# A decoder trunk in float32: the MLP's down projection as a 2x2 block product with seven products

## The chip, the cores and the metric

The kernel is one program on one core of a Trainium2 chip. The core has a tensor engine (PE) with a weight load queue (PEld), a vector engine (DVE), a scalar engine (ACT), a general engine (POOL), and a queue that issues DMAs (SP). The metric is device microseconds of one execution. The kernel before took 1333.41 us, the median of three runs (1332.4 to 1335.83).

## What is computed

Two decoder layers on 512 tokens of width 1024. A layer is a token mixer, an MLP and a gated per-layer embedding:

```
for i in range(2):
    hn = rmsnorm(h, norm_mix_g[i])
    h = h + (even_mixer if i == 0 else odd_mixer)(hn, ...)
    hn = rmsnorm(h, norm_mlp_g[i])
    u = square(relu(hn @ w_mlp_up[i]))       # 512 x 4096
    h = h + u @ w_mlp_down[i]                # 512 x 1024
    gate = sigmoid(rmsnorm(h, norm_ple_g[i]) @ w_ple_gate[i])
    h = h + (p[i] @ w_ple_proj[i]) * gate
return rmsnorm(h, final_norm_g)
```

Everything is float32. The change is in the line with `w_mlp_down`, and in where a few tiles of the other stages lie.

## The kernel before

Activations are kept transposed: eight tiles `h0` to `h7` of 128 features x 512 tokens. Every large product is done in float32r with both operands split into a high and a low part, three matmuls for each pair of 128x128 weights and moving tile (`mm3`): high x high, high x low, low x high. The weights come as 1 MB blocks (`wload`, two buffers `raw`); ACT makes the high part (`wh`, a copy into float32r), DVE the low part (`wl`, the difference), three buffers of 128 x 1024 each. In the mixers POOL makes the low parts instead.

The MLP goes over the hidden width in four chunks of 1024. In a chunk, four *up blocks* each make two hidden tiles of 128 x 512: 48 matmuls of 512 columns into two PSUM banks, then relu and the norm's factor on DVE (L674), the square on ACT (L675), the high part on ACT (L678) and the low part on DVE (L679). Then four *down blocks* each make two tiles of the output: for each tile eight k-steps of `mm3`, 48 matmuls of 512 columns, and DVE adds the bank to `h` (L686). In the last chunk each finished tile is handed on to the next norm (`nxt.done`: split, square, running sum). PSUM has eight banks, taken in turn.

Each engine works its instructions off in the order that the framework's scheduler has put them in when the kernel is built; that order is fixed, and an instruction that waits holds up those behind it on its engine. SP issues the weight blocks in the order of use, each waiting until its `raw` buffer is free. A pool's memory is given to the next pool when the first one closes, and the first writer there waits for the last reader.

The per-layer embedding's projection is computed during the mixer, stored to DRAM (`pjd`) and read back as eight tiles `pj`; before, the pool for them is opened ahead of the MLP, so that these loads stand in front of the MLP's second weight block. The mixer uses scratch tiles `tmp` and `tmp2` and four half-zero tiles `klz`, which before live for the whole kernel.

Of the kernel before, what the change touches and what calls it, by code (L numbers as in the profile page):

```python
# [19 lines left out]
P = 128  # L20
D = 1024
S = 512
# [40 lines left out]
def trunk(  # L63
# [8 lines left out]
    def nm(s):  # L72
        uid[0] += 1
        return f"{s}_{uid[0]}"
# [8 lines left out]
    def const(shape, name, dtype=F32):  # L83
        return cpool.tile(shape, dtype, tag=name, name=name)

    T_BUFS = {"e": 5, "tmp": 1, "tmp2": 3}

    def t2k(tag, pool=None, dtype=F32):
        return (pool or spool).tile([P, S], dtype, tag=tag, name=nm(tag), bufs=T_BUFS.get(tag, 2))

    def col(name="c"):
        return spool.tile([P, 1], F32, tag="col", name=nm(name), bufs=24)
# [9 lines left out]
    def ps_wide():  # L102
        t = ps(wide[wide_i[0] % 8])
        wide_i[0] += 1
        return t
# [45 lines left out]
    def run(units):  # L151
        for _ in units:
            pass
# [204 lines left out]
    klz = [[const([P, S], f"klz{s}{x}", F32R) for x in range(KLB)] for s in range(2)]  # L358
    kl_i = [0]
    for x in range(KLB):  # L360
        nc.gpsimd.memset(klz[0][x][64:128].bitcast(F32), 0.0)
        nc.gpsimd.memset(klz[1][x][0:64].bitcast(F32), 0.0)


    def mixer(layer, norm, nxt):
        st = ExitStack()
        mpool = st.enter_context(tc.tile_pool(name=f"mpool{layer}", bufs=2))
        NSLOT = 13
        pth = [mpool.tile([P, NSLOT, P], F32R, tag=f"pth{i}", name=nm("pth"), bufs=1) for i in range(2)]
        ptl = [mpool.tile([P, NSLOT, P], F32R, tag=f"ptl{i}", name=nm("ptl"), bufs=1) for i in range(2)]  # L370
# [286 lines left out]
        st.close()  # L657


    def mlp(layer, fpool, norm, nxt):  # L660
        ahl = norm.parts()
        rstd = None
        NCH = 4
        for ch in range(NCH):
            uhl = []
            for c in range(4):
                blk = block(w_up[layer, 4 * ch + c], KT, P)
                accs = [ps_wide() for _ in range(2)]
                run(lin_units(accs, blk, ahl, 0, KT, ch == 0 and c == 0))
                if rstd is None:  # L670
                    rstd = norm.finish(use_tables(sig_tail) if layer == 0 else None)
                for acc in accs:
                    u = t2k("u", fpool)
                    nc.vector.scalar_tensor_tensor(u, acc, 0.0, rstd, op0=ALU.max, op1=ALU.mult)  # L674
                    nc.scalar.activation(u, u, AF.Square, scale=0.5)  # L675
                    uh = fpool.tile([P, S], F32R, tag="uh", name=nm("uh"), bufs=12)
                    ul = fpool.tile([P, S], F32R, tag="ul", name=nm("ul"), bufs=12)
                    nc.scalar.activation(uh, u, AF.Copy)  # L678
                    nc.vector.tensor_tensor(ul, u, uh.bitcast(F32), op=ALU.subtract)  # L679
                    uhl.append((uh, ul))  # L680
            for c in range(4):
                blk = block(w_down[layer, 4 * ch + c], KT, P)
                for i in range(2):
                    acc = ps_wide()
                    lin(acc, blk[i][0], blk[i][1], uhl, 0, KT)
                    nc.vector.tensor_tensor(h[2 * c + i], h[2 * c + i], acc, op=ALU.add)  # L686
                    if ch == NCH - 1:
                        nxt.done(2 * c + i)


    def ple_proj(layer, pool):
# [110 lines left out]
    for layer in range(DEPTH):  # L802
        n_mlp, n_ple, n_next = Norm(1, layer), Norm(2, layer), Norm(0, layer + 1)
        mixer(layer, norm, n_mlp)
        with tc.tile_pool(name=f"ppool{layer}", bufs=1) as ppool:
            lo_eng[0] = nc.vector
            pj = ple_proj(layer, ppool)
            with tc.tile_pool(name=f"fpool{layer}", bufs=1) as fpool:
                mlp(layer, fpool, n_mlp, n_ple)
            with tc.tile_pool(name=f"gpool{layer}", bufs=1) as gpool:  # L810
                if layer < DEPTH - 1:
                    ple_t(layer, gpool, pj, n_ple, n_next)
                else:
                    ple_final(layer, gpool, pj, n_ple)
        norm = n_next
        lo_eng[0] = nc.gpsimd


def _pack(w, rows, c0, n, subs, split_rows=False):

    t = np.stack([w[r * P:(r + 1) * P, c0:c0 + n] for r in rows], axis=1)
    if split_rows:
        t = t.reshape(P, subs, len(rows) // subs, n)
    else:
        t = t.reshape(P, len(rows), subs, n // subs).transpose(0, 2, 1, 3)
    return t.reshape(P, -1)


def _feeds(a):
# [3 lines left out]
    for layer, w in enumerate((a["w_in_even"][0], a["w_in_odd"][0])):  # L833
        blocks = []
        for j, g in enumerate(GROUPS[layer]):
# [4 lines left out]
            else:  # L840
# [20 lines left out]
        "w_down": np.array([[_pack(down[l], range(8 * ch, 8 * ch + 8), 256 * c, 256, 2)  # L861
                             for ch in range(4) for c in range(4)] for l in layers]),
# [31 lines left out]
```

## Time and profile before

| | |
|---|---|
| median of three runs | 1333.41 us |
| profiled execution | 1334.15 us, span of the core 1332.4 us, granted clock 0.997 |
| layer 0: mixer, MLP, gate | to about 299 us, to about 647 us, to about 699 us |
| layer 1: mixer, MLP, gate and output | to about 937 us, to about 1273 us, to the end |
| DMA | 133.07 MB, mean 100 GB/s |

The page gives each engine's busy time and its share of the span; the chain of waits follows the work that ended last back from the end; a group of instructions has its line, engine, shapes, count, total busy time and mean duration in ns, and then the idle time before it with what ended it. Durations of matmuls overlap on PE, so the distance from start to start in the timeline is read beside them.

### The profile page before, as it was taken

The page shows a single profiled execution, that of the slowest core. Times are in us where ns is not written, and L with a number is a line of the kernel's source. Part 1 is how long each engine was busy: PE and PEld are TensorE (multiplying, and loading weights), DVE is VectorE, ACT ScalarE, POOL GpSimd, SP SyncE. Part 2 cuts the span into 40 slices and gives each one's busy share as a digit, 9 for nine tenths or more (in the row PEclk, how much of TensorE's full clock was granted, in tenths as well). Part 3 has the DMA queues.
Part 4 walks back from the last instruction along what each step waited for, and adds up shares of the span by engine and source line. Part 5 has one row for each costly group of instructions (what it writes and reads, how often), then busy time and mean ns, then how long its engine had stood idle before and what let it go on. Part 6 is the DMA issues. An engine that isn't in the chain of part 4 may idle for free.

```text
span 1332.4 us, 16447 instructions
## 1 busy us (share of the span) xinstructions
PE 1302.0 (98%) x6360; PEld 1089.0 (82%) x6360; DVE 804.8 (60%) x1389; ACT 631.9 (47%) x1085; POOL 187.2 (14%) x156
## 2 busy tenths in 40 slices
PE   8999999999999999999999999999999999999997
PEld 7878787788888888888889899878888888888886
DVE  6688789865344343345667888887634434434566
ACT  6566768544233132234456667765422313324344
POOL 2333343410000000000004333322000000000001
PEclk9999999999999999999999999999999999999999
DMA  5321323243222222222232232214322222222221
GB/s 205 116 95 56 111 96 104 87 158 111 103 102 95 95 95 95 95 95 95 95 119 99 71 109 74 70 64 148 105 97 97 101 104 102 100 96 95 95 79 64
DMA packets 28031, 133.07 MB, mean 100 GB/s; under 512 B 3312, under 2 KB 4048, under 8 KB 15280
## 3 DMA queue, kind: packets, MB, share of 16 engines
q1 hardware_dynamic: 27952, 132.01, 28.8%
q8 instruction: 50, 0.82, 0.3%
q14 instruction: 29, 0.24, 0.1%
HBM read 125.63 MB, written 6.37 MB: 99 GB/s over the span
## 4 chain that ended last, share of the span: by engine, by line
PE 77%; DVE 14%; ACT 6%; issue 1%; DMA 1%; SPq 0%; ACTq 0%
PE mm L135 12%; PE mm L134 12%; PE mm L136 12%; PE tp L134 5%; PE tp L136 5%; PE tp L135 5%; PE sc L134 5%; PE sc L136 5%; PE sc L135 5%; PE pv L135 3%; PE pv L134 2%; PE pv L136 2%; DVE e L568 2%; PE pv L530 2%; DVE qq L463 1%
## 5 line engine op out<-in xcount | busy, mean ns | idle before, releaser
L120 ACT ACTIVATE wh<-raw 128x1024 fp32r<-128x1024 f32 (+1 forms) x216 | 224.7, 1043 | 497.6 <-PE mm L135 180.4
L134 PE MATMUL mm<-hi,wh 128*128 128x512 f32 x564 | 222.4, 394 | 0.5 <-ACT wh L300 0.4
L124 POOL TENSOR_TENSOR wl<-raw,wh 128x512 fp32r<-128x512 f32 (+1 forms) x132 | 176.5, 1360 | 322.4 <-ACT wh L120 315.8
L135 PE MATMUL mm<-lo,wh 128*128 128x512 f32 x564 | 221.0, 392 | 0.3 <-DVE lo L175 0.3
L136 PE MATMUL mm<-hi,wl 128*128 128x512 f32 x564 | 220.5, 391 | 0.3 <-DVE wl L126 0.3
L126 DVE TENSOR_TENSOR wl<-raw,wh 128x1024 fp32r<-128x1024 f32 x150 | 183.4, 1224 | 44.1 <-ACT wh L120 37.8
L136 PEld LDWEIGHTS mm<-hi,wl 128*128 128x128 f32 x564 | 106.0, 188 | 23.4 <-DVE wl L126 0.7
L134 PEld LDWEIGHTS mm<-hi,wh 128*128 128x128 f32 x564 | 106.1, 188 | 20.7 <-ACT wh L300 0.7
L135 PEld LDWEIGHTS mm<-lo,wh 128*128 128x128 f32 x564 | 106.1, 188 | 20.6 <-DVE lo L175 1.0
L507 ACT ACTIVATE e<-e,mn 128x128 f32<-128x128 f32 (+3 forms) x96 | 53.8, 561 | 52.8 <-DVE mn L504 52.4
L134 PE MATMUL mm<-uh,wh 128*128 128x512 f32 x192 | 74.7, 389 | 0.0
L135 PE MATMUL mm<-ul,wh 128*128 128x512 f32 x192 | 74.7, 389 | 0.0
L136 PE MATMUL mm<-uh,wl 128*128 128x512 f32 x192 | 74.7, 389 | 0.0
L136 PE MATMUL sc<-hi,wl 128*128 128x512 f32 x168 | 65.6, 390 | 0.0
L135 PE MATMUL sc<-lo,wh 128*128 128x512 f32 x168 | 65.4, 389 | 0.0
L134 PE MATMUL sc<-hi,wh 128*128 128x512 f32 x168 | 65.4, 389 | 0.0
L135 PE MATMUL mm<-wl,hi 128*128 128x256 f32 (+1 forms) x216 | 64.6, 299 | 0.4 <-DVE wl L126 0.4
L136 PE MATMUL mm<-wh,lo 128*128 128x256 f32 (+1 forms) x216 | 64.4, 298 | 0.0
L134 PE MATMUL mm<-wh,hi 128*128 128x256 f32 (+1 forms) x216 | 64.3, 298 | 0.0
L780 POOL TENSOR_TENSOR ht<-ht,gb 128x512 f32<-128x512 f32 x4 | 6.3, 1596 | 390.0 <-ACT gt L778 390.0
L686 DVE TENSOR_TENSOR h<-h,mm 128x512 f32<-128x512 f32 x24 | 16.5, 688 | 72.7 <-PE mm L136 72.7
L134 PE MATMUL tp<-hi,wh 128*128 128x512 f32 x152 | 59.1, 389 | 0.0
(218 smaller groups left out, 2883.5 us busy)
## 6 DMA issues: line engine op xcount, KB each, us to landing
raw<-in_w_up_dram SPq DMA_DIRECT2D x32, 1024.0 KB, 4.8
raw<-in_w_down_dram SPq DMA_DIRECT2D x32, 1024.0 KB, 4.9
raw<-in_w_in_dram SPq DMA_DIRECT2D x23, 1024.0 KB, 4.9
raw<-in_w_gate_dram SPq DMA_DIRECT2D x8, 1024.0 KB, 4.9
bias<-urow SPq DMA_DIRECT2D x24, 256.0 KB, 3.2
raw<-in_w_outa_dram SPq DMA_DIRECT2D x8, 768.0 KB, 4.3
pjd<-tmp SPq DMA_DIRECT2D x16, 256.0 KB, 2.3
pj<-pjd SPq DMA_DIRECT2D x16, 256.0 KB, 4.2
```

What stands on the lines that cost most here:

```text
L120: nc.scalar.activation(hi, src, AF.Copy)
L124: nc.gpsimd.tensor_tensor(lo[:, kx], src[:, kx], hi[:, kx].bitcast(F32), op=ALU.subtract)
L126: nc.vector.tensor_tensor(lo, src, hi.bitcast(F32), op=ALU.subtract)
L134: nc.tensor.matmul(acc, lh, rh, start=start, stop=False)
L135: nc.tensor.matmul(acc, lh, rl, start=False, stop=False)
L136: nc.tensor.matmul(acc, ll, rh, start=False, stop=stop)
L463: nc.vector.tensor_tensor(q[b], f[a], q[a].bitcast(F32), op=ALU.subtract)
L507: nc.scalar.activation(e[:, 0:n], e[:, 0:n], AF.Exp, scale=-1.0, bias=mn, accum_out=s)
L530: nc.tensor.matmul(op[:, q0:S], stat(j), mov, start=c == 0, stop=c == nmm - 1)
L568: nc.vector.tensor_tensor_scan(kr, kr, kr, 1.0, op0=ALU.mult, op1=ALU.bypass)
L686: nc.vector.tensor_tensor(h[2 * c + i], h[2 * c + i], acc, op=ALU.add)
L780: nc.gpsimd.tensor_tensor(hk[t][:, 0:512], hk[t][:, 0:512], gb[:, 0:512], op=ALU.mult)
```

## The change

In the first three of the four chunks the down projection is done as a block product. The hidden tiles of one up block (two tiles of 128 features, each with a left and a right half of 256 tokens) are a 2x2 block matrix B; the weights of one down block are, for each of the four up blocks, a 2x2 matrix A of 128 x 128 blocks. Seven products replace eight:

- DVE combines the hidden halves into T1 to T4 (of the four Bs), and the weights into S1 to S4, in float32, before the split. The hidden tile of an up block becomes one tile of seven 256-column pieces (T1, B11, T3, B21, B22, T2, T4); its high and low parts are made in one instruction each. Five such tiles are kept.
- A down block makes the products S1T1, S2T2, S3T3, A11B11, S4B22, A12B21 and A22T4, with moving operands of 256 columns, each 4 x 3 matmuls, in four PSUM banks. The products that reach several outputs (S1T1, S2T2, S3T3, A11B11) are collected over the three chunks in `side` tiles (ACT copies them in the first chunk, DVE adds them in the other two); the others go into `h` at once.
- `side_sums` adds the collected products into the four output blocks, eight DVE instructions of 256 columns for each of the four column blocks, once a layer.
- The order of the blocks is now: the first up block of a chunk, the four down blocks of the chunk before, the other three up blocks. The fourth chunk's down blocks stay as they were, with eight k-steps of 512 columns.
- The host packs the weights of the changed blocks as A12, A22, A21, A11.
- `tmp`, `tmp2` and `klz` now lie in the mixer's pool (so `klz` is zeroed in each layer), and `pj` is loaded in the gate's pool, after the MLP.

The core of the diff; what is left out is marked:

```diff
     def t2k(tag, pool=None, dtype=F32):
-        return (pool or spool).tile([P, S], dtype, tag=tag, name=nm(tag), bufs=T_BUFS.get(tag, 2))
+        return (pool or (mix[0] if tag in ("tmp", "tmp2") else spool)).tile([P, S], dtype, tag=tag, name=nm(tag), bufs=T_BUFS.get(tag, 2))
...
+    T1, B11, T3, B21, B22, T2, T4 = range(7)
...
+            u = fpool.tile([P, 7, HW], F32, tag="u", name=nm("u"), bufs=1)
+            uh = fpool.tile([P, 7, HW], F32R, tag="uh", name=nm("uh"), bufs=5)
+            ul = fpool.tile([P, 7, HW], F32R, tag="ul", name=nm("ul"), bufs=5)
+            for i, acc in enumerate(accs):
+                ui = u[:, B11 + 2 * i:B11 + 2 * i + 2].rearrange("p a c -> p (a c)")
+                nc.vector.scalar_tensor_tensor(ui, acc, 0.0, rstd[0], op0=ALU.max, op1=ALU.mult)
+                nc.scalar.activation(ui, ui, AF.Square, scale=0.5)
+            parts = slice(0, 7)
+            if ch < NCH - 1:
+                nc.vector.tensor_tensor(
+                    u[:, T1:T3 + 1:2], u[:, B11:B22 + 1:3], u[:, T3:T3 + 1].to_broadcast([P, 2, HW]), op=ALU.subtract)
+                nc.vector.scalar_tensor_tensor(
+                    u[:, T2], u[:, T1], -1.0, u[:, B22], op0=ALU.mult, op1=ALU.subtract)
+                nc.vector.scalar_tensor_tensor(
+                    u[:, T4], u[:, T2], -1.0, u[:, B21], op0=ALU.mult, op1=ALU.subtract)
+            else:
+                parts = slice(B11, B22 + 1)
+            nc.scalar.activation(uh[:, parts], u[:, parts], AF.Copy)
+            nc.vector.tensor_tensor(ul[:, parts], u[:, parts], uh[:, parts].bitcast(F32), op=ALU.subtract)
...
+        def down(ch, c):
+            raw = wload(w_down[layer, 4 * ch + c])
+            rv = raw.rearrange("p (s k c) -> p s (k c)", s=4, k=4)
+            A12, A22, S3, A11 = range(4)
+            sums = fpool.tile([P, 3, S], F32, tag="sums", name=nm("sums"), bufs=1)
+            S1, S2, S4 = range(3)
+            nc.vector.tensor_tensor(sums[:, S1], rv[:, S3], rv[:, A22], op=ALU.add)
+            nc.vector.tensor_tensor(sums[:, S2], sums[:, S1], rv[:, A11], op=ALU.add)
+            nc.vector.tensor_tensor(rv[:, S3], rv[:, S3], rv[:, A11], op=ALU.add)
+            nc.vector.tensor_tensor(sums[:, S4], sums[:, S2], rv[:, A12], op=ALU.add)
...
+            def product(bank, half, w, x, t, start, stop):
+                wh, wl = w
+                acc = banks[bank][:, half * HW:half * HW + HW]
+                for k, (uh, ul) in enumerate(us):
+                    mm3(acc, wh[:, x, k], wl[:, x, k], uh[:, t], ul[:, t], start and k == 0, stop and k == 3)
...
+            w = split(sums[:, S1:S2 + 1])
+            product(0, 0, w, 0, T1, True, False)
+            product(0, 1, w, 1, T2, False, True)
+            total(0, 0)
+            w = split(rv[:, S3:A11 + 1])
+            product(1, 0, w, 0, T3, True, False)
+            product(1, 1, w, 1, B11, False, True)
+            total(1, 1)
+            product(2, 1, split(sums[:, S4:S4 + 1]), 0, B22, True, False)
+            w = split(rv[:, A12:A22 + 1])
+            product(2, 0, w, 0, B21, False, True)
+            nc.vector.tensor_tensor(h[2 * c], h[2 * c], banks[2], op=ALU.add)
+            product(3, 0, w, 1, T4, True, True)
+            nc.vector.tensor_tensor(h[2 * c + 1][:, 0:HW], h[2 * c + 1][:, 0:HW], banks[3][:, 0:HW], op=ALU.subtract)
...
+        for c in range(4):
+            up(0, c)
+        for ch in range(1, NCH):
+            up(ch, 0)
+            for c in range(4):
+                down(ch - 1, c)
+            for c in range(1, 4):
+                up(ch, c)
+                if ch == NCH - 1:
+                    side_sums(c)
+        side_sums(0)
+        for c in range(4):
+            down_last(c)
...
-        with tc.tile_pool(name=f"ppool{layer}", bufs=1) as ppool:
-            lo_eng[0] = nc.vector
-            pj = ple_proj(layer, ppool)
-            with tc.tile_pool(name=f"fpool{layer}", bufs=1) as fpool:
-                mlp(layer, fpool, n_mlp, n_ple)
-            with tc.tile_pool(name=f"gpool{layer}", bufs=1) as gpool:
...
+        lo_eng[0] = nc.vector
+        with tc.tile_pool(name=f"fpool{layer}", bufs=1) as fpool:
+            mlp(layer, fpool, n_mlp, n_ple)
+        with tc.tile_pool(name=f"gpool{layer}", bufs=1) as gpool:
+            pj = ple_proj(layer, gpool)
...
```

How this moves instructions, at three places. In the rows a name is a buffer with its number, what is written to the left of the arrow, what is read to the right.

PE in a down block of layer 0. Before, the first matmuls of the first chunk's first block (`mm_3513` is a bank, `wh_3505` and `wl_3506` the weights' parts, `uh`, `ul` those of the hidden tiles):

```order
L134 MATMUL mm_3513<-uh_3208,wh_3505 128x512
L135 MATMUL mm_3513<-ul_3209,wh_3505 128x512
L136 MATMUL mm_3513<-uh_3208,wl_3506 128x512
L134 MATMUL mm_3513<-uh_3215,wh_3505 128x512
L135 MATMUL mm_3513<-ul_3216,wh_3505 128x512
L136 MATMUL mm_3513<-uh_3215,wl_3506 128x512
```

Now, in a block of the second chunk, where one product ends and the next begins:

```order
L136 MATMUL mm_4481<-uh_4159,wh_4557 128x256
L137 MATMUL mm_4481<-ul_4160,wh_4557 128x256
L138 MATMUL mm_4481<-uh_4159,wl_4558 128x256
L136 MATMUL sc_4482<-uh_3483,wh_4557 128x256
L137 MATMUL sc_4482<-ul_3484,wh_4557 128x256
L138 MATMUL sc_4482<-uh_3483,wl_4558 128x256
```

The matmuls are half as wide, and a block has 84 instead of 48; the order on PE is otherwise that of the program.

DVE in a run of down blocks. Before, in layer 0's second chunk, low parts of weights and adds into `h` take turns:

```order
L686 TENSOR_TENSOR h_91<-h_91,pv_4021 128x512
L126 TENSOR_TENSOR wl_4112<-raw_4109,wh_4111 128x1024
L686 TENSOR_TENSOR h_92<-h_92,mm_4057 128x512
L126 TENSOR_TENSOR wl_4116<-raw_4109,wh_4115 128x1024
L686 TENSOR_TENSOR h_93<-h_93,mm_4083 128x512
```

Now, in the third chunk, between the second and the third block (`wl_5229` is the low part of the third block's first pair, `side` and L766 are the side totals and the side sums, L713 a weight sum of the fourth block):

```order
L766 TENSOR_TENSOR h_90<-h_90,side_3113 128x256
L742 TENSOR_TENSOR side_3114<-side_3114,sc_5109 128x512
L726 TENSOR_TENSOR wl_5229<-sums_5219,wh_5228 128x1024
L726 TENSOR_TENSOR e_5287<-sums_5219,e_5286 128x512
L766 TENSOR_TENSOR h_90<-h_90,side_3112 128x256
L742 TENSOR_TENSOR side_3115<-side_3115,tp_5110 128x512
L766 TENSOR_TENSOR h_91<-h_91,side_3113 128x256
L726 TENSOR_TENSOR wl_5258<-raw_5217,wh_5257 128x1024
L713 TENSOR_TENSOR sums_5334<-raw_5332 128x512
```

The low parts of the next block stand behind the side totals of the block that PE is at, and the side sums of the first column blocks are put between them rather than after the run.

SP at the end of layer 0's MLP. Before:

```order
L112 DMA raw_5476<-in_w_gate_dram 128x2048
L112 DMA raw_5560<-in_w_gate_dram 128x2048
L112 DMA raw_5644<-in_w_gate_dram 128x2048
L112 DMA raw_5750<-in_w_in_dram 128x2048
L112 DMA raw_5810<-in_w_in_dram 128x2048
```

Now:

```order
L114 DMA raw_6189<-in_w_gate_dram 128x2048
L797 DMA pj_5993<-pjd 128x512
L797 DMA pj_5995<-pjd 128x512
L797 DMA pj_5997<-pjd 128x512
L797 DMA pj_5999<-pjd 128x512
L797 DMA pj_6001<-pjd 128x512
L797 DMA pj_6003<-pjd 128x512
L797 DMA pj_6005<-pjd 128x512
L797 DMA pj_6007<-pjd 128x512
L114 DMA raw_6273<-in_w_gate_dram 128x2048
L114 DMA raw_6386<-in_w_in_dram 128x2048
```

The eight loads of `pj`, which stood ahead of the MLP's second weight block, now stand between the third and the fourth block of the gate's weights.

More of the change, by code (lines that the diff above doesn't have):

```diff
@@ L367, in mixer @@
         mpool = st.enter_context(tc.tile_pool(name=f"mpool{layer}", bufs=2))
+        mix[:] = [mpool]
+        klz = [[mpool.tile([P, S], F32R, tag=f"klz{s}{x}", name=nm("klz"), bufs=1) for x in range(KLB)]
+               for s in range(2)]
+        for x in range(KLB):
+            nc.gpsimd.memset(klz[0][x][64:128].bitcast(F32), 0.0)
+            nc.gpsimd.memset(klz[1][x][0:64].bitcast(F32), 0.0)
         NSLOT = 13
@@ L657, in mixer @@
         st.close()
+    HW = S // 2
+    T1, B11, T3, B21, B22, T2, T4 = range(7)
     def mlp(layer, fpool, norm, nxt):
         ahl = norm.parts()
-        rstd = None
+        rstd = []
         NCH = 4
-        for ch in range(NCH):
-            uhl = []
-            for c in range(4):
[L667 to L688, printed above, removed]
@@ new lines, in mlp, with up @@
+        sides = [[fpool.tile([P, S], F32, tag=f"side{x}{c}", name=nm("side"), bufs=1) for x in range(2)] for c in range(4)]
+        hidden = {}
+        def up(ch, c):
+            blk = block(w_up[layer, 4 * ch + c], KT, P)
+            accs = [ps_wide() for _ in range(2)]
+            run(lin_units(accs, blk, ahl, 0, KT, ch == 0 and c == 0))
+            if not rstd:
+                rstd.append(norm.finish(use_tables(sig_tail) if layer == 0 else None))
+            u = fpool.tile([P, 7, HW], F32, tag="u", name=nm("u"), bufs=1)
[17 more added lines that the diff above has]
+            nc.vector.tensor_tensor(ul[:, parts], u[:, parts], uh[:, parts].bitcast(F32), op=ALU.subtract)
+            hidden[ch, c] = (uh, ul)
@@ new lines, in down_last @@
+        def down_last(c):
+            blk = block(w_down[layer, 4 * (NCH - 1) + c], KT, P)
+            uhl = [tuple(x[:, B11 + 2 * i:B11 + 2 * i + 2].rearrange("p a c -> p (a c)") for x in hidden[NCH - 1, k])
+                   for k in range(4) for i in range(2)]
+            for i in range(2):
+                acc = ps_wide()
+                lin(acc, blk[i][0], blk[i][1], uhl, 0, KT)
+                nc.vector.tensor_tensor(h[2 * c + i], h[2 * c + i], acc, op=ALU.add)
+                nxt.done(2 * c + i)
```

45 lines of the change are left out of this document (35 added, 10 removed).

## The prediction

> **What bounds the kernel now.** I read the page first (busy shares, then the chain of waits), then a stretch of the MLP in the view by stages, then the timeline of TensorE, because the page warns that a busy PE is not PE at its peak.
>
> ```profile
> PE 1302.0 (98%) x6360; PEld 1089.0 (82%) x6360; DVE 804.8 (60%) x1389; ACT 631.9 (47%) x1085; POOL 187.2 (14%) x156
> PE 77%; DVE 14%; ACT 6%; issue 1%; DMA 1%; SPq 0%; ACTq 0%
> raw<-in_w_down_dram SPq DMA_DIRECT2D x32, 1024.0 KB, 4.9
> 331.00:508.00 177.00, 177.00 (x783) 146.56 (x782) 72.07 (x81) 53.03 (x65) 0.00 (x0) 1.00 0.29 100
> ```
>
> The last row is a stage wholly inside layer 0's MLP; its columns are the length, then busy time of PE, PEld, DVE, ACT and POOL, the granted clock, DMA share and GB/s. PE is busy 177.00 of 177.00 us at clock 1.00; DVE and ACT are busy 72 and 53 us, and POOL does nothing. Nothing but PE sets the time here. So the change is worth what it does to PE's time, as long as DVE and ACT, which get more work, stay behind cover. Of the 32 blocks of the down projection, 24 change (three chunks of four column blocks, two layers).
>
> The trap is the duration of a matmul. By shapes, and then as starts in the timeline (columns: start, duration):
>
> ```profile
> L136 PE MATMUL mm<-uh,wl 128*128 128x512 f32 x192 | 74.7, 389 | 0.0
> L136 PE MATMUL sc<-wh,lo 128*128 128x256 f32 x32 | 9.1, 283 | 0.0
> 339.77 0.39 PE L135 MATMUL pv<-ul,wh 128*128 128x512 f32 x1
> ...
> 349.97 0.39 PE L135 MATMUL mm<-ul,wh 128*128 128x512 f32 x1
> 39.76 0.28 PE L134 MATMUL sc<-wh,hi 128*128 128x256 f32 x1
> ...
> 44.68 0.28 PE L136 MATMUL tp<-wh,lo 128*128 128x256 f32 x1
> ```
>
> Going by durations, a 256-column matmul would cost 283/389 = 0.73 of a 512-column one. But they overlap: from 339.77 to 349.97 lie 45 steps, 226.7 ns each; from 39.76 to 44.68 lie 41 steps, 120.0 ns each. What counts is the step. Two points give a line: (226.7 - 120.0)/256 = 0.417 ns per column and 13.3 ns per matmul whatever its width. The 256-column matmuls of that stretch (the first value projection) are built as the new ones will be: a fresh 128x128 float32r stationary operand each, one bank half as target.
>
> **The change part by part.**
>
> *PE.* A changed block went through 2 accumulators x 8 k x 3 = 48 matmuls of 512 columns: 48 x 226.7 = 10.88 us. Now it goes through 7 products x 4 k x 3 = 84 of 256 columns: 84 x 120.0 = 10.08 us. In the two terms of that line: 3072 columns less at 0.417 ns save 1.28 us, and 36 more fixed costs of 13.3 ns take 0.48 back. The saving is 0.80 us a block, **24 x 0.80 = 19.2 us**. Bounds of the 120 ns: below, half of 226.7 (no fixed cost), 113.3, saving 1.36 x 24 = 32.6 us; above, the break-even is 10.88/84 = 129.5 ns, only 8% off, so this number carries the forecast. I take 120.0, the row of the same form.
>
> [...]
>
> *DVE and ACT, does the cover hold?* Prices:
>
> ```profile
> L126 DVE TENSOR_TENSOR wl<-raw,wh 128x1024 fp32r<-128x1024 f32 x150 | 183.4, 1224 | 44.1 <-ACT wh L120 37.8 <-PE tp L242 6.3
> L679 DVE TENSOR_TENSOR ul<-u,uh 128x512 fp32r<-128x512 f32 x64 | 44.1, 691 | 0.0
> L686 DVE TENSOR_TENSOR h<-h,mm 128x512 f32<-128x512 f32 x24 | 16.5, 688 | 72.7 <-PE mm L136 72.7
> L520 DVE TENSOR_TENSOR ptl<-tp,pth 128x256 fp32r<-128x256 f32 x28 | 11.5, 412 | 0.5 <-ACT pth L519 0.5
> L120 ACT ACTIVATE wh<-raw 128x1024 fp32r<-128x1024 f32 x200 | 211.2, 1059 | 496.2 <-PE mm L135 179.1 <-PE tp L135 114.5 <-PE sc L135 108.5
> L678 ACT ACTIVATE uh<-u 128x512 fp32r<-128x512 f32 x64 | 40.5, 633 | 2.0
> L675 ACT ACTIVATE u<-u 128x512 f32<-128x512 f32 x64 | 39.6, 619 | 8.8 <-DVE u L674 8.8
> ```
>
> A changed down block on DVE: four weight sums 4 x 0.69, three low parts of 1024 columns 3 x 1.22, one of 512 0.69, two side totals 2 x 0.69 (in the first chunk ACT copies them), h adds 0.69 + 0.41: 9.6 us (8.2 in the first chunk), was 3.8. ACT: 3 x 1.06 + 0.63 = 3.8 us. An up block of the first three chunks on DVE: 2 x 1.22 + 2 x 0.69, combinations 0.69 + 2 x 0.41, low part of 1792 columns, 2.02 by the slope of the first two rows: 7.4 us, was 5.2. So an up and a down block together hold 17.0 us of DVE under 20.96 us of PE. On average the cover holds; inside a run of four down blocks it is tight, 9.6 under 10.08, and the extra work of the up block before it falls there too.
>
> So I followed the queue by hand, in the order shown, through the hardest run: the third chunk's four down blocks, where the order also places the side sums (8 x 0.41 a block). T = 0 is the first of their matmuls; a product takes 12 x 0.12 = 1.44 us. A weight buffer of three is refilled when the two products that read it are over, so a pair of the next block can be split 7.2 us before PE wants it, and the split takes 1.06 (ACT) + 1.22 (DVE): 4.9 us of margin. DVE starts with the tail of the up block (relu, low part of 1024; done at 4.1). It reaches the low part of the second block's first pair at 5.9 (wanted at 10.1), of the third block's at 15.6 (20.2), of the fourth's at 26.1 (30.2), of the next up block's first half at 37.3 (40.3) and of its second at 40.3 (45.8). Margins shrink from 4.9 to 3.0 us and never reach nothing. The walk lets a DVE instruction start up to 0.08 us before its predecessor's duration is over, as these two do (1.19 us apart at 1.23 long):
>
> ```profile
> 399.77 1.23 DVE L126 TENSOR_TENSOR wl<-raw,wh 128x1024 fp32r<-128x1024 f32 x1 [0.17 <-ACT wh L120]
> 400.96 0.69 DVE L679 TENSOR_TENSOR ul<-u,uh 128x512 fp32r<-128x512 f32 x1
> 404.35 0.69 DVE L674 SCALAR_TENSOR_TENSOR u<-mm,rstd 128x512 f32<-128x512 f32 x1 [2.69 <-PE mm L136]
> ```
>
> With full durations one after another the smallest margin is about 1.9 us. So the cover costs nothing at these durations. If it goes, DVE sets the pace (below). Below nothing the edit cannot go: PE has no idle time there to win.
>
> *Last up block to first plain down block.* The last hidden tile is now made in one piece of 1024. After its last matmul: relu 0.69, ACT's weight split 1.06 beside it, square 0.62, high part 1.06, low part 1.22, about 4.1 us. PE wants the high part after 18 matmuls, 4.08 us, the low part one step later. Even; at most 0.5 us a layer. I take 0.
>
> *PLE reload.* The eight loads of pj move on SP's queue from before the MLP to after the third gate load, and wait there for the MLP's last matmul; behind them stands the fourth gate load (in layer 1 also the final gain and the last two gate loads).
>
> ```profile
> L695 SPq DMA_DIRECT2D pj<-pjd x16: 326/431/1469, 270.6 to 913.0; - x16
> L713 DVE TENSOR_TENSOR gt<-gt,pj x8: 679/684/692, 655.2 to 685.9; 128x512 f32<-128x512 f32 x8
> DMA to landing us min/median/max: 3.0/4.2/6.7
> 1279.61 4.99 SPq L112 DMA_DIRECT2D raw<-in_w_gate_dram  x2
> 1285.31 1.06 ACT L120 ACTIVATE wh<-raw 128x1024 fp32r<-128x1024 f32 x1 [6.19 <-PE tp L136]
> ```
>
> Eight issues take 8 x 0.43 = 3.5 us; the last lands 7 to 11 us after the last down matmul. The first is wanted after a gate block of PE (48 x 0.227 = 10.9 us) and the norm behind it, so it is hidden; the fourth gate load is wanted 33 us on. In layer 1 the two gate loads of 1279.61 may land some 4 us later and delay the split of 1285.31, whose weights serve the second half of the gate, after 96 x 0.227 = 22 us. 0, at most 1.5 us.
>
> *Mixer scratch and klz.* Four memsets are added on POOL at the start of layer 1, ahead of the value weights' splits:
>
> ```profile
> L361 POOL MEMSET klz<- 64x512 f32 x2 | 1.0, 520 | 0.1
> 687.75 0.35 POOL L372 MEMSET ptl<- 128x128 f32 x2
> 694.49 2.57 POOL L124 TENSOR_TENSOR wl<-raw,wh 128x512 fp32r<-128x512 f32 x2 [6.38 <-ACT wh L120]
> ```
>
> 4 x 0.52 = 2.1 us into 6.38 us in which POOL waits for ACT: 0. The scratch tiles keep their number of buffers: 0.
>
> *Sum.* The profiled execution took 1334.15 us with a span of 1332.4; the median of the runs is 1333.41, 0.7 less. 1333.4 - 19.2 = **1314.2 us**.
>
> **The rivals.** The bound of faster and slower is 0.3%, 4.0 us, about what a measurement of this kernel tells from no change.
>
> *Part of the gain is given back in stalls.* The four or six runs of down blocks eat their margin at the seams and PE waits 1 to 2.3 us in each of six: 6 to 14 us, so 1320 to 1328. For it: the margins of 1.9 to 3.0 us above come from a count by hand. Against: every run before it has more room, and up blocks leave DVE 3.5 us each to recover.
>
> *DVE becomes the bound (slower).* Place: the low parts in the down runs. In DVE's order the side totals and h adds wait for PE, and the low parts behind them wait with them. It decides once a down block takes DVE over 10.08 us, 5% above my sum, for longer than the margin lasts. Price, with nothing of it hidden by the lead: in the second chunk's run 4 x 9.6, the up block's tail 0.69 + 0.69 + 0.82 + 2.02 and the next up block's split 2.45 make 45.1 us against 40.3 of PE; in the third chunk's 4 x 9.6 + 1.9 + 2.45 and the side sums, 13.2, make 56.0. Over by 4.8 + 15.7 us a layer, 41 us in all: 1314 + 41 = 1355; half of it 1335. If the adds ran as slowly as these, it would be far more:
>
> ```profile
> L472 DVE TENSOR_TENSOR klz<-tmp,kh 64x512 fp32r<-64x512 f32 x32 | 32.8, 1025 | 8.5 <-ACT kh L470 8.2
> ```
>
> at 1.49 times 0.69, a block takes 13.1 us and 24 x (13.1 - 10.88) = +53, 1387. Those ran while POOL was at work; in the MLP POOL has x0, and L679 takes 691.
>
> *The step of a 256-column matmul is not 120 ns here.* If PE could not overlap weight loads with such short matmuls, each pair would cost its load:
>
> ```profile
> L136 PEld LDWEIGHTS mm<-hi,wl 128*128 128x128 f32 x564 | 106.0, 188 | 23.4 <-DVE wl L126 0.7
> ```
>
> 84 x 0.188 = 15.8 us a block, +118 us, 1451. Against: the stretch at 39.76 had a load per matmul too. [...]
>
> *More is saved:* a step nearer 117 or 113 ns, 1301 to 1308.
>
> **How the numbers follow.** Forecast (1308 to 1319) 0.67; stalls (1320 to 1328) 0.15; DVE bound (1329 to 1355) 0.10; a dearer step 0.03; more saved 0.05. Faster needs less than 1329.4: 0.86; within: 0.07; slower: 0.07. The range runs from 1306 to 1327.
>
> **What would show it.** PE should hold 7224 matmuls, with starts 120 ns apart in the down runs and idle under 5 us more than before; DVE about 1010 us busy (805 and 24 x 5.8 - 8 x 1.4, 24 x 2.2, 8 x 3.3); PE waits released by DVE's low parts at L726 absent. Waits there, or a step above 125 ns, would make the prediction wrong.

## The result and the profile after

The changed kernel takes 1315.14 us, the median of four runs (1313.5 to 1315.48); the kernel before, on the same chip, 1334.62 us (1332.4 to 1336.32). The ratio is 0.9853, with an interval of 0.9834 to 0.9871. The forecast was 1314.2 us. The profiled execution took 1313.5 us with a span of 1311.6; that of before had a span of 1332.4.

Two lines of the page of the changed kernel, engines and chain of waits:

```profile
PE 1280.7 (98%) x7224; PEld 1112.5 (85%) x7224; DVE 982.5 (75%) x1669; ACT 686.4 (52%) x1117; POOL 189.0 (14%) x160
...
PE 78%; DVE 12%; ACT 7%; issue 2%; DMA 1%; SPq 0%; ACTq 0%; DVEq 0%
```

DVE has 178 us more work than before and 15 points more of the span, yet its share of the chain has fallen from 14% to 12%, a first sign that the added work is not on the path. The view by stages says where it went. Its rows are the three runs of four changed down blocks in layer 0; the columns are length, busy time of PE, PEld, DVE, ACT and POOL, granted clock, DMA share and GB/s:

```profile
342.27:382.59 40.32, 40.32 (x338) 40.31 (x337) 28.50 (x35) 20.16 (x25) 0.00 (x0) 1.00 0.32 109
426.13:466.45 40.32, 40.32 (x338) 40.31 (x337) 33.83 (x43) 16.09 (x16) 0.00 (x0) 1.00 0.33 109
509.99:550.31 40.32, 40.32 (x338) 40.31 (x337) 39.31 (x66) 15.39 (x16) 0.00 (x0) 1.00 0.32 109
```

PE is busy for the whole of each run, even of the third, in which DVE is busy 39.31 us of 40.32. The same stretch of before, the four plain down blocks of the third chunk:

```profile
507.51:551.02 43.51, 43.51 (x193) 36.03 (x192) 15.97 (x17) 9.64 (x11) 0.00 (x0) 1.00 0.28 97
```

So four blocks take 40.31 us from first start to next start instead of 43.52, and six such runs give 6 x 3.21 = 19.3 us. The four up blocks between two runs take 43.55 us instead of 43.52. The rest of the 20.8 us between the two spans is not the change's: the profiled execution of before ran 3.41 us at half clock in its first mixer, and that of the changed kernel did not:

```profile
48.60:52.01 3.41, 3.41 (x19) 3.41 (x18) 2.29 (x8) 0.29 (x2) 2.32 (x2) 0.50 0.45 173
```

A 256-column step takes 0.213 us there (12 steps from 49.02 to 51.58) instead of 0.120, so the stretch holds 16 of them instead of 28 and costs 1.5 us. 19.3 - 0.2 + 1.5 = 20.6 of the 20.8. The granted clock of the changed kernel's four executions lies between 0.996 and 0.999, so the executions differ in their time at half clock; the medians are 19.5 us apart.

The step, and the margin that DVE keeps, from the timeline of the changed kernel (start, duration), in the second run: a low part of the second block and its first reader, then where that block ends and the third begins:

```profile
434.63 1.22 DVE L726 TENSOR_TENSOR wl<-raw,wh 128x1024 fp32r<-128x1024 f32 x1
...
439.33 0.28 PE L138 MATMUL tp<-uh,wl 128*128 128x256 f32 x1
...
445.81 0.28 PE L138 MATMUL pv<-uh,wl 128*128 128x256 f32 x1
...
446.77 0.28 PE L137 MATMUL mm<-ul,wh 128*128 128x256 f32 x1
```

From 445.81 to 446.77 lie eight steps, 120 ns each. The low part of the second block's second pair of weights is ready at 435.85 and first read at 439.33, 3.5 us later; this is the smallest such margin of all six runs (for the third block's first pair it is 4.4 us, in the third chunk's run nowhere under 4.2).

### The profile page after: what moved, and what is told of

Same layout as the page of the kernel before. It is cut to its first block, busy times and chain, and to the rows that moved or that the text cites. A ratio compares the mean times of both kernels' runs of the same rounds, so it can differ in the third digit from the quotient of the medians.

```text
span 1311.6 us, 18552 instructions
## 1 busy us (share of the span) xinstructions
PE 1280.7 (98%) x7224; PEld 1112.5 (85%) x7224; DVE 982.5 (75%) x1669; ACT 686.4 (52%) x1117; POOL 189.0 (14%) x160
## 4 chain that ended last, share of the span: by engine, by line
PE 78%; DVE 12%; ACT 7%; issue 2%; DMA 1%; SPq 0%; ACTq 0%; DVEq 0%
PE mm L137 12%; PE mm L138 12%; PE mm L136 12%; PE tp L138 5%; PE tp L136 5%; PE tp L137 5%; PE sc L136 4%; PE sc L137 4%; PE sc L138 4%; PE pv L137 2%; PE pv L136 2%; PE pv L138 2%; PE pv L534 2%; DVE e L572 2%; PE tp L519 1%
## 5 line engine op out<-in xcount | busy, mean ns | idle before, releaser
L122 ACT ACTIVATE wh<-raw 128x1024 fp32r<-128x1024 f32 (+1 forms) x168 | 173.5, 1037 | 230.1 <-PE mm L137 72.6
L725 ACT ACTIVATE wh<-raw 128x1024 fp32r<-128x1024 f32 x48 | 50.7, 1057 | 70.7 <-PE sc L137 35.5
L138 PE MATMUL mm<-uh,wl 128*128 128x256 f32 (+1 forms) x288 | 86.6, 301 | 0.0
L137 PE MATMUL mm<-ul,wh 128*128 128x256 f32 (+1 forms) x288 | 86.6, 301 | 0.0
L136 PE MATMUL mm<-uh,wh 128*128 128x256 f32 (+1 forms) x288 | 86.6, 301 | 0.0
L704 DVE TENSOR_TENSOR ul<-u,uh 128x1792 fp32r<-128x1792 f32 (+1 forms) x32 | 58.4, 1824 | 23.4 <-ACT uh L703 23.4
L703 ACT ACTIVATE uh<-u 128x1792 fp32r<-128x1792 f32 (+1 forms) x32 | 49.4, 1543 | 48.4 <-DVE u L699 48.2
L692 ACT ACTIVATE u<-u 128x512 f32<-128x512 f32 x64 | 39.4, 624 | 53.4 <-DVE u L691 53.4
```

The costliest lines, as they stand in the source:

```text
L122: nc.scalar.activation(hi, src, AF.Copy)
L136: nc.tensor.matmul(acc, lh, rh, start=start, stop=False)
L137: nc.tensor.matmul(acc, lh, rl, start=False, stop=False)
L138: nc.tensor.matmul(acc, ll, rh, start=False, stop=stop)
L692: nc.scalar.activation(ui, ui, AF.Square, scale=0.5)
L703: nc.scalar.activation(uh[:, parts], u[:, parts], AF.Copy)
```

## The experiments

### The two parts that are not products

First what is left when the products are taken out. One kernel is the one before with only the memory moves (mixer scratch and `klz` in the mixer's pool, `pj` loaded in the gate's pool):

```diff
...
-        with tc.tile_pool(name=f"ppool{layer}", bufs=1) as ppool:
-            lo_eng[0] = nc.vector
-            pj = ple_proj(layer, ppool)
...
+        with tc.tile_pool(name=f"gpool{layer}", bufs=1) as gpool:
+            pj = ple_proj(layer, gpool)
...
```

> The kernel before with the moves alone: mixer scratch and the half-zero tiles in the mixer's pool, the pj loads behind the MLP; the MLP as before. My theory: no part of the gain, 1333 to 1336 us, within 2 us of the kernel before. Rival (the moved loads or the added memsets cost or win something): 3 us or more either way.

Measured: 1333.87 us, ratio 0.9998 (0.9989 to 1.0008). The moves neither give nor cost.

The other is the kernel before with only the new order of the blocks:

```diff
-        for ch in range(NCH):
-            uhl = []
...
+        for c in range(4):
+            up(0, c)
+        for ch in range(1, NCH):
+            up(ch, 0)
             for c in range(4):
...
+                down(ch - 1, c)
+            for c in range(1, 4):
+                up(ch, c)
+        for c in range(4):
+            down(NCH - 1, c)
```

> The kernel before, with the new order of the blocks (up block 0 of the next chunk ahead of the four down blocks of this one) and nothing else: the down blocks stay plain, 48 matmuls of 512 columns. My theory (the gain is the 24 x (48 x 226.7 - 84 x 120.0) ns of PE and nothing of the order): 1332 to 1336, equal to before within 0.3%. Rival (the order spares PE waits at the four seams of each layer, and so makes part of the gain): 1325 to 1331.

Measured: 1334.01 us, ratio 0.9998 (0.9989 to 1.0008). With plain down blocks the order is worth nothing: before, too, PE had no wait in the MLP that the order could spare.

### One product more

An eighth product, A22T4 once more into the unread half of its bank; its result is not used.

```diff
-            product(3, 0, w, 1, T4, True, True)
+            product(3, 0, w, 1, T4, True, False)
+            product(3, 1, w, 1, T4, False, True)
```

> An eighth product a changed block (A22 T4 once more, into the unread right half of the fourth bank): 96 matmuls of 256 columns instead of 84, DVE and ACT unchanged. My theory (PE sets the time, 120 ns a matmul): 24 x 12 x 0.120 = +34.6 us over the changed kernel, 1349 to 1350 us, so slower than the kernel before by 15 us: eight half-wide products lose to the old form. Rival (part of PE's time in the changed kernel is waiting for DVE): the added PE time hides some of it, +20 us or less, 1335 or below.

Measured: 1349.41 us, ratio 1.0119 (1.0103 to 1.0134); a down run takes 46.07 us instead of 40.31. That is 384 steps of 120 ns, and 6 x 5.76 = 34.6 us in all; the medians lie 34.3 apart. A product of 12 matmuls costs its 12 steps in full, 1.44 us, so nothing but PE sets these runs. It also shows how thin the exchange is: with eight products of 256 columns the kernel is slower than with plain blocks.

### How much DVE can take

Extra adds of 512 columns on DVE in every changed down block, two or six; their results are not used.

```diff
+            spare = fpool.tile([P, S], F32, tag="spare", name=nm("spare"), bufs=1)
+            for _ in range(2):
+                nc.vector.tensor_tensor(spare, sums[:, S1], sums[:, S2], op=ALU.add)
```

With two:

> Two more DVE adds of 512 columns a changed block, into a scratch tile that nothing reads: 11.0 us of DVE under 10.08 us of PE. My theory (3 to 5 us of margin in each run of four blocks): 4 x 1.4 = 5.5 us more a run, of which the margin takes most; 0 to 3 us of waiting a run where the margin is short, 1315 to 1324 us. Rival (DVE already sets the pace in the runs): 24 x 1.38 = +33 us, 1348.

Measured: 1314.24 us, ratio 0.9856 (0.984 to 0.9872), the same as the changed kernel and 0.8 us under my range, since not even the 0 to 3 us of waiting that I allowed a run came. Its third run, in the view by stages:

```profile
510.18:550.50 40.32, 40.32 (x338) 40.31 (x337) 40.09 (x64) 15.44 (x16) 0.00 (x0) 1.00 0.33 109
```

DVE is busy 40.09 of 40.32 us and PE has not lost a step. With six:

> Six more DVE adds of 512 columns a changed block, into a scratch tile that nothing reads: 13.7 us of DVE under 10.08 of PE, so DVE must set the pace. My theory: six runs of four blocks, each over by 4 x 3.7 (less 1.4 a block in the first chunk, more by the side sums in the third) less 3 to 5 us of margin, about 66 us together, 1365 to 1395 us, with waits of PE that DVE's low parts of the weights end. Rival (DVE already sets the pace): 24 x 4.14 = +99 us, 1414.

Measured: 1336.45 us, ratio 1.0014 (1.0004 to 1.0023): 21 us lost, not 50 to 80. The first two runs of layer 0 (40.31 us each in the changed kernel), and, in the whole kernel, what PE waited for there:

```profile
343.76:385.70 41.94, 40.83 (x337) 40.42 (x336) 41.23 (x58) 21.00 (x26) 0.00 (x0) 1.00 0.31 103
429.25:475.15 45.90, 43.66 (x337) 42.23 (x336) 44.12 (x64) 16.66 (x18) 0.00 (x0) 0.96 0.25 90
```

```profile
PE sc L136 <- ACT wh L729: 4.3, 8, 1.1
...
PE tp L136 <- ACT wh L729: 2.4, 4, 0.7
```

Here DVE is the bound, as the mechanism has it: from the first run to the end of the second ACT's splits wait 17.4 us for the weight sums of L714 on DVE, and PE waits for the splits. (The clock of 0.96 in the second run is one stretch at half clock, some 1.5 us of the loss.) But my price for DVE was too high. I had added up durations, 9.6 us a block and 13.7 with six adds. The timeline of this kernel shows that durations on DVE overlap as they do on PE:

```profile
441.83 0.68 DVE L720 TENSOR_TENSOR spare<-sums 128x512 f32<-128x512 f32 x1
442.44 0.68 DVE L746 TENSOR_TENSOR side<-side,sc 128x512 f32<-128x512 f32 x1
443.03 0.68 DVE L720 TENSOR_TENSOR spare<-sums 128x512 f32<-128x512 f32 x1
...
444.84 1.22 DVE L730 TENSOR_TENSOR wl<-raw,wh 128x1024 fp32r<-128x1024 f32 x1
```

0.68 us long, they start 0.60 us apart; for 1024 columns the step is about 1.14, and for 256 about 0.34. By steps a changed block is 4 x 0.60 + 3 x 1.14 + 0.60 + 2 x 0.60 + 0.60 + 0.34 = 8.6 us, 9.8 with two adds (still under 10.08) and 12.2 with six. Part of the adds also went into the up stretches, and the lead took up some.

### Narrower still

Every 256-column matmul of a changed block as two of 128, each with its own load of the same weights; the result is the same.

```diff
-                    mm3(acc, wh[:, x, k], wl[:, x, k], uh[:, t], ul[:, t], start and k == 0, stop and k == 3)
+                    for y in range(2):
+                        yy = slice(y * P, (y + 1) * P)
+                        mm3(acc[:, yy], wh[:, x, k], wl[:, x, k], uh[:, t, yy], ul[:, t, yy],
+                            start and k == 0 and y == 0, stop and k == 3 and y == 1)
```

> The changed kernel with every 256-column matmul of the down blocks as two of 128 columns (168 in a block, the same weights loaded for each). It tells what sets the step. If it is linear in columns with 13.3 ns a matmul, as from 512 to 256: 66.7 ns a matmul, 11.2 us a block, 24 x 1.12 = 27 us more, 1342. If below 256 columns the load of the 128 x 128 weights sets the step (the loads' busy time is 154 ns in the mean in the page of the changed kernel, and they ran at 120 ns without a gap, so a floor lies anywhere up to 120): at 107 to 120 ns 18.0 to 20.2 us a block, 1505 to 1557.

Measured: 1524.39 us, ratio 1.142 (1.1397 to 1.1443). Two matmuls of one down run, eight steps apart, in the timeline:

```profile
379.80 0.28 PE L137 MATMUL tp<-ul,wh 128*128 128x128 f32 x1
...
380.69 0.28 PE L136 MATMUL tp<-uh,wh 128*128 128x128 f32 x1
```

A run of 672 takes 74.99 us, 111.6 ns a matmul, not 66.7. The line of the prediction through 226.7 and 120.0 ns does not hold down to 128 columns. That halving the columns leaves 111.6 of 120.0 ns fits a floor by the weight load (in the timeline of PEld the loads start 0.11 us apart, at 379.85, 379.96 and 380.07); that it is the load and not another cost of each matmul was not separated. The 107 ns at which the expectation lets the floor begin was my estimate, and no run shows it. The 120 ns on which the gain rests stands 8.4 ns above this step.

### The order of the blocks, with the products

The changed kernel with the order of before: four up blocks, then the four down blocks that read them.

```diff
-        for c in range(4):
-            up(0, c)
-        for ch in range(1, NCH):
-            up(ch, 0)
+        for ch in range(NCH):
             for c in range(4):
-                down(ch - 1, c)
-            for c in range(1, 4):
                 up(ch, c)
-                if ch == NCH - 1:
+                if ch == NCH - 1 and c:
                     side_sums(c)
+            if ch < NCH - 1:
+                for c in range(4):
+                    down(ch, c)
```

> The changed kernel, all its seven products, with the order of the blocks from before: the four up blocks of a chunk, then its four down blocks, so that no up block of the next chunk stands between the last up block and the products that read its splits. With seven products in the last chunk too, where nothing stood between either, PE waited 1.2 and 1.3 us there for the two splits of the last up block and 3.3 us for a weight split behind them on DVE, and ran at half clock for 3.4 us once or twice (1.7 us each). Theory (the up block in between, 10.9 us of PE, is what hides the chain from the last up block to the products): 2.5 to 6 us of waits and 1.7 to 3.4 of half clock at each of the six down runs with products, 25 to 56 us over the changed kernel, so 1340 to 1371, more than the whole gain gone. Rival (the order does nothing, as with plain down blocks): 1313 to 1318.

Measured: 1349.5 us, ratio 1.0118 (1.0099 to 1.0137), 34 us over the changed kernel and slower than before. The timeline at the second run's start, whose first matmul is at 424.82:

```profile
425.64 0.68 DVE L691 SCALAR_TENSOR_TENSOR u<-tp,rstd 128x512 f32<-128x512 f32 x1
...
429.07 1.70 ACT L703 ACTIVATE uh<-u 128x1792 fp32r<-128x1792 f32 x1 [2.08 <-DVE u L699]
...
430.80 2.03 DVE L704 TENSOR_TENSOR ul<-u,uh 128x1792 fp32r<-128x1792 f32 x1 [1.82 <-ACT uh L703]
...
430.82 0.38 PE L136 MATMUL tp<-uh,wh 128*128 128x256 f32 x1 [1.53 <-ACT uh L703]
...
432.88 0.38 PE L137 MATMUL tp<-ul,wh 128*128 128x256 f32 x1 [1.32 <-DVE ul L704]
```

The last hidden tile passes through a long chain before PE can read all of it: the second relu at 425.64, the square, three instructions for the combinations, the high part of its seven pieces (1792 columns), the low part. It is ready 8 us after the last up matmul, and PE, which does the first three of the four k-steps of the block's first products meanwhile, then waits for both parts. Over the whole kernel, where the changed one has no such row at all:

```profile
PE tp L136 <- ACT uh L703: 13.6, 6, 3.5
PE tp L137 <- DVE ul L704: 8.0, 7, 1.3
```

That is 21.6 us. Most of the rest is the clock. The runs of this kernel in the view by stages:

```profile
333.02:381.27 48.25, 43.56 (x337) 42.85 (x336) 31.54 (x37) 20.86 (x26) 0.00 (x0) 0.93 0.28 92
424.82:469.98 45.16, 42.31 (x338) 41.90 (x336) 34.07 (x43) 16.27 (x17) 0.00 (x0) 0.96 0.30 99
513.52:559.81 46.29, 42.48 (x337) 41.86 (x336) 39.94 (x63) 17.28 (x18) 0.00 (x0) 0.96 0.28 94
977.54:1026.25 48.71, 43.47 (x337) 42.76 (x336) 31.69 (x37) 21.23 (x27) 0.00 (x0) 0.93 0.26 90
1069.80:1113.22 43.42, 40.81 (x337) 40.40 (x336) 33.80 (x43) 16.20 (x16) 0.00 (x0) 1.00 0.30 102
1156.77:1201.67 44.90, 42.09 (x337) 41.68 (x336) 39.14 (x61) 16.23 (x17) 0.00 (x0) 0.96 0.29 98
```

They add up to 276.7 us against 6 x 40.31 = 241.9 in the changed kernel: 34.9 us. PE is idle for 22.0 us of them (length less busy time), nearly all of it these two waits. The granted clock of 0.93 is two stretches of 3.41 us at half clock in a run, 0.96 is one; there are seven in all. At half clock a step takes 0.213 us (13 from 434.21 to 436.99) instead of 0.120, which costs a stretch up to 1.5 us, less where PE also waits in it: at most 10.5 us. 22.0 + 10.5 = 32.5 of the 34.9; the rest lies in longer steps at the waits, such as the 0.22 us behind 430.82 and behind 432.88.

So the gain belongs to the products and the order together, and to neither alone (medians, each beside runs of the kernel before on its chip):

| | order of before | new order |
|---|---|---|
| plain down blocks | 1334.6 us | 1334.0 us, 0.9998 |
| seven products | 1349.5 us, 1.0118 | 1315.1 us, 0.9853 |

### Seven products in the fourth chunk too

The changed kernel with the last chunk's down blocks as products, whose side sums and hand-on to the next norm then follow in that same run.

```diff
-            if ch < NCH - 1:
+            if True:
...
+                if ch == NCH - 1:
+                    side_sums(c)
...
-            down_last(c)
+            down(NCH - 1, c)
+            side_sums(c)
+            for i in range(2):
+                nxt.done(2 * c + i)
...
```

> The changed kernel with the seven products in the last chunk too; its side sums and the hand-on to the next norm then follow in the last down run. PE has 8 x 0.80 = 6.4 us less. DVE, by the steps from start to start seen in the traces (0.60 us for 512 columns, 1.135 for 1024, 0.335 for 256): a block of seven products 8.5, its eight side sums 2.7, the hand-on of two tiles 2.5, in sum 13.7 us against 10.08 of PE; four such blocks are 14.5 us over, less a lead of some 5. So by the theory that DVE is what limits a fourth chunk: 1322 to 1333, and PE idle in the last down run of each layer for 5 to 10 us, ended by DVE or by ACT's splits. Rival (DVE's lead and the idle time after the run take it up): 1308 to 1311.

Measured: 1347.16 us, ratio 1.0099 (1.0081 to 1.0118), 14 us above my upper bound. The last down run of each layer, which in the changed kernel takes 43.52 us:

```profile
584.18:640.86 56.68, 45.95 (x340) 43.89 (x339) 49.66 (x81) 23.58 (x29) 0.00 (x0) 0.94 0.22 76
1222.65:1283.16 60.51, 48.67 (x341) 46.79 (x339) 48.33 (x82) 21.55 (x27) 0.00 (x0) 0.89 0.20 70
```

PE idles 10.7 and 11.8 us in them (expected 5 to 10), and the clock of 0.94 and 0.89 stands for two and four stretches at half clock, up to 3 and 6 us more, which I had not counted. The two runs are 30.2 us longer, the span 34.4; most of the rest lies in the gate and the output behind the second, 54.5 us from the first start of a matmul to the last against 50.7. Some pieces of the chain of waits in the first of them (start, length):

```profile
588.08 1.71 ACT uh L703
589.81 2.04 DVE ul L704
591.89 0.39 PE tp L137
...
594.84 1.23 DVE wl L726
...
599.07 0.34 DVE side L766
599.40 1.14 DVE wl L726
...
606.05 0.70 DVE e L726
606.79 0.39 PE sc L138
```

Until 591.89 it is the same chain as in the kernel with the order of before: there is no further up block to put ahead. From 594.84 to 606.75 the chain lies on DVE alone, with the low parts that PE wants standing between side sums and hand-on. So the theory held in its mechanism, and failed in the lead: I had let DVE start 5 us ahead, and it starts behind.

The same with the last chunk's four weight sums on POOL, which is idle in the MLP:

```diff
-            nc.vector.tensor_tensor(sums[:, S1], rv[:, S3], rv[:, A22], op=ALU.add)
+            sum_eng = nc.gpsimd if ch == NCH - 1 else nc.vector
+            sum_eng.tensor_tensor(sums[:, S1], rv[:, S3], rv[:, A22], op=ALU.add)
...
```

> As the kernel with seven products in all four chunks, with the weight sums S1 to S4 of the last chunk on POOL, which does nothing in the MLP. DVE then has 13.7 - 2.4 = 11.3 us a block against 10.08 of PE: 5 us over in four blocks, about the lead that it has. Theory (DVE limits the fourth chunk, POOL's adds cost it nothing): 1309 to 1317, and at least 6 us under the one with the sums on DVE. Rival 1 (POOL's adds, 1.36 us each by its adds elsewhere, come too late for the first product of a block, or slow DVE's): 1320 to 1333, no better than on DVE. Rival 2 (DVE was never the limit): both at 1308 to 1311.

Measured: 1363.12 us, ratio 1.0216 (1.02 to 1.0232), 16 us worse than with the sums on DVE. My theory falls, and rival 2 with it; rival 1 has the direction, but not the size. In its timeline, late in the last run of layer 0, DVE's adds of 256 columns while POOL adds (four in a row, from 629.68 to 635.34):

```profile
629.68 1.41 POOL L714 TENSOR_TENSOR sums<-raw 128x512 f32<-128x512 f32 x1 [10.41 <-DVE e L727]
629.84 0.42 DVE L758 TENSOR_TENSOR h<-h,mm 128x256 f32<-128x256 f32 x1
630.17 1.20 DVE L767 TENSOR_TENSOR side<-side,side 128x256 f32<-128x256 f32 x1
...
631.41 1.40 DVE L767 TENSOR_TENSOR h<-h,side 128x256 f32<-128x256 f32 x1
```

L758 reads one operand from PSUM and keeps its 0.42 us; L767 reads both from SBUF and takes as long as an add of POOL.

To see this where DVE is covered, the changed kernel with the weight sums of all 24 changed blocks on POOL:

```diff
-            nc.vector.tensor_tensor(sums[:, S1], rv[:, S3], rv[:, A22], op=ALU.add)
+            nc.gpsimd.tensor_tensor(sums[:, S1], rv[:, S3], rv[:, A22], op=ALU.add)
...
```

> The changed kernel with the four weight sums of every block of seven products on POOL instead of DVE. With them on POOL in the last chunk, DVE's 256-column adds took 1.39 instead of 0.42 us while an add of POOL ran. By that, DVE wins 4 x 0.60 us a block and loses up to 4 x 1.0, at most 1.6 us a block on 8.5: DVE stays near 10.08 in the worst block and the lead takes up the rest: 1314 to 1325, with more busy time on DVE than in the changed kernel's down runs. Rival (POOL's adds cost DVE nothing): 1313 to 1316, with 9.6 us less busy on DVE in each down run of 40.31 us (about 19, 24 and 30 instead of 28.5, 33.8 and 39.3).

Measured: 1380.05 us, ratio 1.0346 (1.033 to 1.0363), 65 us worse than the changed kernel. Both expectations were far too low. Its second run in the view by stages, ACT's longest wait in it, and the timeline around its start:

```profile
438.38:490.12 51.74, 44.92 (x338) 43.68 (x337) 32.47 (x38) 17.40 (x19) 14.90 (x10) 0.93 0.26 87
```

```profile
ACT e L725 <- POOL sums L716: 21.8, 3, 9.5
```

```profile
434.79 1.30 POOL L713 TENSOR_TENSOR sums<-raw 128x512 f32<-128x512 f32 x1 [7.94 <-DVE u L699]
...
436.60 2.73 DVE L704 TENSOR_TENSOR ul<-u,uh 128x1792 fp32r<-128x1792 f32 x1 [1.83 <-ACT uh L703]
437.41 3.08 POOL L715 TENSOR_TENSOR raw<-raw 128x512 f32<-128x512 f32 x1
440.45 1.29 POOL L716 TENSOR_TENSOR sums<-sums,raw 128x512 f32<-128x512 f32 x1
```

DVE has 9.6 us of adds less in a run, yet its busy time fell only from 33.83 to 32.47 us; in 51.74 us that is no bound. The four sums of a block form a chain of 7.0 us from 434.79 to 441.74 (four DVE steps are 2.4), ACT's split of S4 waits for its end, and the splits behind it on ACT wait too. Where both engines are at work, instructions of either take longer: DVE's 2.02 us of L704 become 2.73 beside POOL's adds, and POOL's L715, 1.30 us at 457.32, takes 3.08 at 437.41, its first 1.92 us beside L704. Not every one does: L714 on POOL, beside L704 from 436.60 on, keeps its 1.29 us. The granted clock of the six runs is 0.90 to 0.96, twelve stretches at half clock in all, so up to 18 of the 65 us are the clock's. How much of the rest is the longer chain and how much the longer instructions was not separated.

## Why the prediction was right

- **PE alone bounds these stages, before and after.** Right: 40.32 of 40.32 us busy in each run, and one product more cost its 1.44 us a block in full.
- **The step, not the duration.** Right: 120.0 ns in the new form, 10.08 us a block, 19.3 us against 19.2 forecast. By durations the change would have come out as a loss. The two-point line held where the forecast used it, and not below: 111.6 ns at 128 columns, where it gives 66.7.
- **DVE's cover.** Right in its result, mis-sized in its terms, by durations once more. A changed block is 8.6 us of DVE by steps, not 9.6, and DVE's busy time in the whole kernel is 982.5 us, not about 1010. The walk began with a margin of 4.9 us and let it shrink to 3.0 in the third chunk, which it took for the hardest run; there the least one measured is 4.2, and the least of all, 3.5, is in the second chunk, which the walk did not follow. The price for slow adds is mis-added too: 1.49 times on all but the three low parts of 1024 columns makes 12.5 us of the 9.6 us block, not 13.1; no run showed such adds in the MLP with POOL idle. Two adds more a block are free, and six take all of the gain. Of the two rivals that rest on DVE, stalls at the seams did not come at all, and of the loads tried DVE became the bound at 12.2 us a block and not at 9.8.
- **What the walk did not name.** The 4.9 us were taken from an order that was given, and the text never said what the order itself is worth. It is worth the whole gain: without the up block ahead of each run the same products lose 34 us to waits for the last hidden tile and to the clock. The forecast was right because the new order stood in the change.
- **The small terms** (first plain block, `pj`, scratch and `klz`) at 0: right. There is no wait of PE in the MLP, and the memory moves alone make 0.9998. Behind the final down block, the matmuls span 50.70 us against 50.66.

## What to carry to other kernels

Count engine time by the distance from start to start, on DVE as on PE; durations of neighbours overlap, and here they had the sign of the change wrong on PE and its cover too thin on DVE. A product scheme that trades matmuls for sums needs other matmuls between the sums and their use: ask for each such chain which block of PE hides it, and price the order of the blocks together with the products, since either alone showed nothing or a loss. An engine that is idle is not free if a chain through it gets longer (the four sums of a block took 7.0 us on POOL, four DVE steps are 2.4), or if its work slows the busy one, as POOL's adds did here (DVE's adds with both operands in SBUF took 1.20 to 1.40 us instead of 0.42).

## What the runs showed of the hardware

- **Short gaps cost twice here.** The granted clock was 0.50 in stretches of 3.41 us. Below, the stretch with the two waits in the kernel with the order of before and the one behind it; then a stretch of the kernel with six adds; then one in the first mixer of the kernel before:

```profile
430.41:433.82 3.41, 1.68 (x12) 1.48 (x13) 2.03 (x1) 0.35 (x1) 0.00 (x0) 1.00 0.35 147
433.82:437.23 3.41, 3.41 (x19) 3.41 (x18) 1.53 (x2) 1.06 (x1) 0.00 (x0) 0.50 0.02 5
```

```profile
461.39:464.81 3.42, 2.11 (x11) 1.49 (x12) 3.42 (x7) 2.57 (x4) 0.00 (x0) 1.00 0.13 55
```

```profile
103.22:106.63 3.41, 1.60 (x14) 1.39 (x12) 3.35 (x8) 0.94 (x4) 0.51 (x1) 1.00 0.00 0
```

  In the stretches behind 430.41 and 461.39 the clock was 0.50, in the one behind 103.22 it was 1.00. PE's busy time does not order the three: 1.68 and 2.11 us were followed by half clock, 1.60 was not. The number of matmuls, all of 256 columns, does: 12 and 11 against 14. Whether that number is the cause, and how other widths count, is not shown here. The longest gap of PE ahead of the half clock was 1.53 us in the kernel with the order of before; in the one with six adds all idle time of PE in the stretch was 1.31 us (3.42 less 2.11), in the stretch from 103.22, with full clock behind it, 1.81 us (3.41 less 1.60).
- **A step of 111.6 ns** for a matmul in float32r with its own load of 128 x 128 weights, at 128 columns, where the two wider forms lead to 66.7.
- **Instructions of POOL and DVE took longer beside each other** in the kernels with weight sums on POOL: DVE's adds of 256 columns with both operands in SBUF 1.20 to 1.40 us instead of 0.42, while the one with an operand in PSUM kept 0.42; DVE's L704 2.73 instead of 2.02; POOL's L715 3.08 instead of 1.30, while L714 kept 1.29.
